# Nineteen taps of a depthwise convolution moved from VectorE to ScalarE products and accumulating transfers, in a two-layer encoder on one core

## The chip, the cores and the metric

The kernel runs on 1 core of one Trainium2 chip. The metric is device microseconds (us) of one execution, less is better. The kernel before takes 1756.23 us, the median of 3 runs (1755.57 to 1756.38).

## The reference, cut to what matters

Two layers of an encoder over 512 tokens of 1024 channels, in float32. Each layer projects the normalized tokens, runs three token mixers side by side (a: differential attention with 4 heads, b: a Conformer convolution module, c: neighbourhood attention with 8 heads), weighs each mixer's output by a sigmoid gate, adds the three, and goes on with an output projection, a SwiGLU feed-forward block and a gated embedding. The two places that the change touches are the convolution and the sum of the branches:

```python
def conformer_conv(u, conv_w, conv_b, cln_g, cln_b):
    a, g = jnp.split(u, 2, axis=-1)
    z = a * jax.nn.sigmoid(g)
    z = lax.conv_general_dilated(
        z, conv_w.astype(z.dtype), window_strides=(1,),
        padding=[(CONV_W // 2, CONV_W // 2)],
        dimension_numbers=('NWC', 'WIO', 'NWC'),
        feature_group_count=CB)
    z = z + conv_b
    z = layernorm(z, cln_g, cln_b)
    return jax.nn.silu(z)
...
        merged = (ga * (ya @ w_br_a[i]) + gb * (yb @ w_br_b[i])
                  + gc * (yc @ w_br_c[i]))
```

The convolution has 31 taps (`CONV_W`) and one weight for each tap and channel, over 512 channels (`CB`). The channels lie on the partitions in 4 blocks of 128, so one tap of one block is one pass over a 128x512 tile: multiply a shifted view of the block by a column of weights and add it to the sum. A layer has 4 x 31 = 124 such passes.

## The kernel before, in words

**Products on TensorE.** Activations lie with channels on the partitions and 512 tokens along the free side. A float32 product is made of three matmuls of halves: each weight tile `wr` is loaded by SyncE, ScalarE copies its high part to `wh` (helper `act`, L143), VectorE subtracts to get the low part `wl` (helper `tt`, L157), and `mm3` (L179, L180, L181) issues high x high, high x low, low x high. `weights` does the loading and splitting with raised priority, up to 400 steps ahead of its use; `wr`, `wh` and `wl` have three buffers each.

**Order.** TensorE's order is the program's order, written out by hand (`manual_schedule`). The streams of the other engines are put in order when the kernel is built, by priority and an estimate of when each instruction's inputs are there; a link that is only an order (`NoSync`) holds an instruction behind another one. Within an engine instructions run in that fixed order, and an instruction that waits holds all that are behind it. Attention units (`natten_unit`, `diff_unit`) are put between the projections by counting matmul chunks (`tick`, `later`): a unit's scores (L800) go to two PSUM buffers `sc`; VectorE takes the maximum (L893), ScalarE the exponential of both tiles (`diff_a`, `diff_e`, L143), VectorE mixes them (L898 and L160), and three ticks later TensorE transposes the result.

**The taps.** `taps` is a generator over the 124 passes; each `yield` is one VectorE `scalar_tensor_tensor` (helper `stt`, L160) or, for a block's first tap, one `tensor_scalar` (L551). `background(after, n)` takes the next `n` of them and puts them behind the instruction `after`. `BG` tells how many go where: 4 in the stage `glu`, 8 in `natten`, 12 in the neighbourhood values, 8 in `diff`, 16 in `gatec`, 16 in `branchc`, 16 behind the four first gates of b, and 48 in `mergea` (6 for each of 8 blocks), which is 80 places before `mergea` and 128 in all. What is left is done at the start of `conv`, which adds the four sums, and normalizes them over the channels.

**Stages of a layer around the change.** `diff_in` for heads 0 to 3 projects q and k of one head each: ScalarE copies the PSUM result to `raw` (tile `diff_rp`), four SyncE transfers rotate it, VectorE applies the rotary tables, ScalarE and VectorE split it, SyncE transfers stack it. `gate_c` projects one of 8 gate blocks and copies it (tile `gatec_x`); block 0 stands between heads 1 and 2, blocks 1 to 7 behind head 3. Then `branch_c` (gate times product of branch c, in place in `acc`), `merge_a` (gate of a times product of branch a into `g`, then `acc += g`, two VectorE instructions per block), `conv` with the rest of the gates of b, and `merge_b`, which is the next to read `acc`.

**Transfers that add.** The feed-forward block has them already: two for each of its 44 weight blocks, issued from GpSimd (`accum_op=ALU.add`, L979), which add 128x512 weights from HBM to a tile in SBUF. GpSimd has little else to do: the power -0.5 of the norms (L225, L1334).

**The buffers that the change uses.** Tiles of tag `z` are as large as 128x1024, so a 128x512 sum fills half of one. The tag `rb` has one buffer, which holds a norm's factor for all tokens; between the start of the layer and the convolution's norm it is free.

Of the kernel before, what the change touches and what calls it, by code (L numbers as in the profile page):

```python
# [14 lines left out]
AF = mybir.ActivationFunctionType  # L15
ALU = mybir.AluOpType
# [4 lines left out]
P = 128  # L21
# [3 lines left out]
GR = 8  # L25
# [4 lines left out]
CB = 512  # L30
CON3W = 31
HALO = CON3W // 2
NA_KR = 8
NA_KC = 16
NW = 256
# [10 lines left out]
PAR_L = 8 + 8 + 8 + 1 + 4 + 4 + 4 + 4 * CON3W  # L46
PAR = L * PAR_L + 8
WARM = 8
BG = dict(glu=2, natten=1, values=3, diff=1, gatec=2, branchc=2, gateb=4, mergea=4, mergea2=2)
FIRST = (["v"] * 4 + ["pt"] * 2 + ["y", "b"], ["y"] * 5 + ["pt"] * 2 + ["b"])  # L50
EARLY = 6
QUARTERS = (2, 4, 6)
# [9 lines left out]
class Net:  # L62
# [371 lines left out]
    def layer(self, i, h, xsrc, xs):  # L434
        self.i, self.h = i, h
        zs, cs = [], []
        self.todo = self.taps(zs, cs)
        self.glu(zs)
        if i == 0:
            self.lambdas()  # L440
        yc, ya, yb = [], [], []
        sn, sd = {}, {}
        self.natten_in(0, sn, yc)
        self.drain(self.renorm)
        self.h = self.hs
        self.natten_v(sn)
        last = self.glu_last(zs)
        self.natten_in(1, sn, yc)
        next(last)
        self.natten_in(2, sn, yc)  # L450
        next(last)
        self.natten_in(3, sn, yc)
        acc, gb = [], []
        self.diff_in(0, sd, ya)
        self.diff_v(0, sd)
        self.diff_in(1, sd, ya)
        self.gate_c(acc, 0)
        self.diff_in(2, sd, ya)
        self.diff_v(1, sd)
        self.diff_in(3, sd, ya)  # L460
        for m in range(1, KD):
            self.gate_c(acc, m)
        for m in range(2):
            self.gate_b(gb, m, AF.Copy, None)
        for g in acc + gb:
            self.act(g, g, AF.Sigmoid, table="sigmoid")
        self.branch_c(acc, yc)
        for m in range(2, 4):
            self.gate_b(gb, m, AF.Sigmoid, "sigmoid")
        self.merge_a(ya, acc)  # L470
        conv = self.run(self.conv(cs, yb))
        pairs = self.inputs()
        for m in range(4, KD):
            self.gate_b(gb, m, AF.Sigmoid, "sigmoid")
            for n in ((0, 1), (2,), (3,), ())[m - 4]:
                self.input_block(pairs, n)
        self.drain(conv)
        mg = self.merge_b(yb, acc, gb)
        ws = self.pair_weights(4)
        x, h = self.w_o(mg, xsrc)  # L480
        self.input_pair(ws, pairs, 4)
        h = self.ffn(h, x)
        return self.ple(h, x, xs, self.inputs())
# [8 lines left out]
    def glu(self, zs):  # L492
# [5 lines left out]
        for j in range(3):  # L498
            sg, ta = self.sb("t", [P, 512]), self.sb("t", [P, 512])
            z = self.sb("z", [P, GW + 2 * HALO, GR])  # L500
            zs.append(z)
# [17 lines left out]
    def gated(self, z, a, g):  # L519

        nc = self.nc
        zc = self.tt(z[:, HALO:HALO + GW, :].rearrange("p a b -> p (a b)"), a, g, ALU.mult)
        nc.vector.memset(z[:, 0:HALO, 0:1], 0.0)
        nc.vector.memset(z[:, HALO + GW:, GR - 1:GR], 0.0)
        nc.vector.tensor_copy(z[:, 0:HALO, 1:GR], z[:, GW:GW + HALO, 0:GR - 1])
        nc.vector.tensor_copy(z[:, HALO + GW:, 0:GR - 1], z[:, HALO:2 * HALO, 1:GR])
        return zc
# [13 lines left out]
    def taps(self, zs, cs):  # L541

        for j, z in enumerate(zs):
            zf = z.rearrange("p a b -> p (a b)")
            c = self.sb("z", [P, 512])
            cs.append(c)
            for d in range(CON3W):
                w = self.par(self.i, "cw", j * CON3W + d)
                src = zf[:, d * GR:d * GR + 512]
                if d == 0:  # L550
                    yield self.nc.vector.tensor_scalar(c, src, w, self.par(self.i, "cb", j),  # L551
                                                       ALU.mult, ALU.add)
                else:
                    yield self.stt(c, src, w, c, ALU.mult, ALU.add)

    def background(self, after, n):

# [193 lines left out]
    def gate_c(self, acc, m):  # L751
        self.phase = "gatec"
        ps = self.proj(OFF_G + 2 * D + m * P)
        if m % 2 == 0:
            acc += self.parts_of("x", [512], 2)
        self.background(self.act(acc[m], ps, AF.Copy), self.bg["gatec"])

    def branch_c(self, acc, ys):
        self.phase = "branchc"
        for m in range(KD):  # L760
            ps = self.ps("mm")
            self.gemm(ps, self.a["w_br_c"][self.i, m], ys)
            self.background(self.tt(acc[m], acc[m], ps, ALU.mult), self.bg["branchc"])

    def merge_a(self, ys, acc):
        self.phase = "mergea"
        for m in range(KD):
            ps = self.proj(OFF_G + m * P)
            g = self.sb("t", [P, 512])
            self.background(self.act(g, ps, AF.Sigmoid, table="sigmoid"), self.bg["mergea"])  # L770
            pb = self.ps("mm")
            self.gemm(pb, self.a["w_br_a"][self.i, m], ys)
            self.tt(g, g, pb, ALU.mult)
            self.background(self.tt(acc[m], acc[m], g, ALU.add), self.bg["mergea2"])

    def gate_b(self, gs, m, func, table):
        self.phase = "gateb"
# [24 lines left out]
    def diff_in(self, head, st, ys):  # L802
        self.phase = "diff"
        if head == 0:
            st["tabs"] = []
            for t in range(2):
                c = self.sb("r", [P, 512])
                self.nc.sync.dma_start(c, self.a["rope"][t])
                st["tabs"].append(c)
        st4 = self.sb("qk", [P, 4, 512], F32R)  # L810
        k2 = self.sb("x", [P, 2, 512], F32R)
        for s, off in enumerate((OFF_QA, OFF_KA)):
            ps = self.proj(off + head * P)
            raw, rot = self.sb("rp", [P, 512]), self.sb("rp", [P, 512])
            self.act(raw, ps, AF.Copy, scale=1.0 if s else 0.125)
            for b in range(4):
                o = b ^ 1
                self.nc.sync.dma_start(rot[32 * b:32 * b + 32], raw[32 * o:32 * o + 32])
            t = self.sb("t", [P, 512])
            self.background(self.tt(t, raw, st["tabs"][0], ALU.mult), self.bg["diff"])  # L820
            self.tt(rot, rot, st["tabs"][1], ALU.mult)
            self.tt(t, t, rot, ALU.add)
            nat, low = self.sb("kh", [P, 512], F32R), raw.bitcast(F32R)
            self.split(nat, low, t)
            self.stack(nat, low, st4[:, 2 * s:2 * s + 2], k2 if s else None)
        box = dict(s0=self.sb("sm", [P, 4]))
        for qt in range(4):
            self.later(self.diff_unit(head, qt, st4, k2, st, box, ys), 6 if head else 7, 2)
# [693 lines left out]
```

## Time and profile before

| | before |
|---|---|
| median of 3 runs | 1756.23 us |
| the profiled execution's own time | 1756.09 us |
| its span, from the first to the last instruction | 1754.3 us |
| PE, matmuls | 1747.3 us busy, 8970 instructions |
| PEld, weight loads | 1490.2 us busy |
| DVE (VectorE) | 1421.7 us busy, 81% |
| ACT (ScalarE) | 964.4 us busy, 55% |
| POOL (GpSimd) | 104.0 us busy, 6% |
| mean granted clock of TensorE | 0.999 |

The profiled execution lies 0.14 us under the median, and its span leaves 1.8 us of its time uncovered. A row of a timeline reads: start in us from the span's start, duration in us, engine, line, operation, output tile and inputs, shape, count; in square brackets, the idle time of the engine just before and who ended it. In a view by tile the three durations are minimum, median and maximum in ns. Matmul rows are modelled at their ends and overlap: the distance from one start to the next tells TensorE's pace, not the duration. In the rows of windows the numbers after an engine are busy us and instructions.

### The profile page before, as it was taken

Reading aid. Unit: us, or ns where it says so; the run is one execution under the profiler, and the core shown is the slowest. Engines: PE = TensorE matmul, PEld = TensorE weight load, DVE = VectorE, ACT = ScalarE, POOL = GpSimd, SP = SyncE. Lnnn points to the kernel's source line nnn. Section 1 sums busy time; section 2 is a strip of 40 time slices with the busy share of each in tenths; the row PEclk is TensorE's granted clock in tenths of the full one; section 3 lists DMA queues with packets and bytes.
Section 4 is the critical chain, followed back from the end, with each engine's and each line's share of the span. In section 5 each row is a group of like instructions: output and inputs, shape, how many; then the busy total and the mean of one; then the engine's idle time right before and its main releaser. Section 6 shows DMA issues by size and latency. Waiting matters only on the chain.

```text
span 1754.3 us, 25072 instructions
## 1 busy us (share of the span) xinstructions
PE 1747.3 (100%) x8970; PEld 1490.2 (85%) x8970; DVE 1421.7 (81%) x2346; ACT 964.4 (55%) x1729; POOL 104.0 (6%) x114
## 2 busy tenths in 40 slices
PE   9999999999999999999999999999999999999998
PEld 7888888888888888888888898888888988888887
DVE  7967987998799687797776688889887985977876
ACT  5566545226577275574545665553365763745654
POOL 0000000000121020100000000000001210101000
PEclk9999999999999999999999999999999999999999
DMA  6575641334767365543446655323256764755332
GB/s 230 159 192 158 162 126 46 112 100 140 230 162 186 118 171 155 142 119 131 156 130 164 194 150 153 111 73 96 93 176 199 183 172 121 179 143 157 96 105 97
DMA packets 114781, 253.82 MB, mean 145 GB/s; under 512 B 16864, under 2 KB 23776, under 8 KB 114656
## 3 DMA queue, kind: packets, MB, share of 16 engines
q1 hardware_dynamic: 101264, 227.83, 42.3%
q0 software_dynamic: 12672, 23.07, 8.1%
q8 instruction: 71, 1.16, 0.3%
q10 hardware_dynamic: 720, 1.31, 0.2%
q14 instruction: 54, 0.44, 0.1%
HBM read 215.46 MB, written 7.34 MB: 127 GB/s over the span
## 4 chain that ended last, share of the span: by engine, by line
PE 97%; DVE 1%; DMA 1%; ACT 1%; SPq 0%; issue 0%; POOL 0%; POOLq 0%; ACTq 0%; DVEq 0%
PE ffn_mm L1013 6%; PE ffn_sc L1013 6%; PE ffn_mm L180 4%; PE ffn_mm L179 4%; PE ffn_mm L181 4%; PE ffn_mm L1016 3%; PE ffn_sc L1016 3%; PE mergea_mm L180 2%; PE mergea_mm L181 2%; PE mergea_mm L179 2%; PE ffn_tr L1013 2%; PE natten_mm L179 2%; PE natten_mm L180 2%; PE gateb_mm L180 2%; PE gateb_mm L181 2%; PE gateb_mm L179 2%
## 5 line engine op out<-in xcount | busy, mean ns | idle before, releaser
L160 DVE SCALAR_TENSOR_TENSOR conv_z<-glu_z,pre_par,conv_z 128x512 f32<-128x512 f32 x240 | 179.6, 748 | 3.4
L143 ACT ACTIVATE ffn_wh<-ffn_wr 128x1024 fp32r<-128x1024 f32 (+1 forms) x92 | 92.7, 1021 | 99.5 <-PE ffn_mm L180 63.4
L157 DVE TENSOR_TENSOR ffn_wl<-ffn_wr,ffn_wh 128x1024 fp32r<-128x1024 f32 (+1 forms) x92 | 107.1, 1175 | 20.8 <-ACT ffn_wh L143 20.4
L979 POOL DMA_DIRECT2D ffn_qk<-w_fu x88 | 78.0, 992 | 589.3 <-DMA ffn_qk<-w_fu 323.7
L143 ACT ACTIVATE mergea_wh<-mergea_wr 128x1024 fp32r<-128x1024 f32 (+1 forms) x32 | 27.1, 846 | 96.8 <-PE mergea_mm L180 79.6
L157 DVE TENSOR_TENSOR ffn_t<-ffn_mm,wo_rb 128x512 f32<-128x512 f32 (+1 forms) x46 | 31.1, 677 | 51.6 <-PE ffn_mm L181 51.6
L157 DVE TENSOR_TENSOR ffn_wl<-ffn_qk,ffn_wh 128x1024 fp32r<-128x1024 f32 x44 | 53.7, 1220 | 11.0 <-ACT ffn_wh L143 10.9
L143 ACT ACTIVATE diff_a<-diff_sc,diff_s 128x512 f32<-128x512 f32 x32 | 22.0, 688 | 71.6 <-DVE diff_s L893 71.6
L143 ACT ACTIVATE ffn_wh<-ffn_qk 128x1024 fp32r<-128x1024 f32 x44 | 46.7, 1061 | 26.8 <-PE ffn_mm L180 16.2
L179 PE MATMUL ffn_mm<-ffn_v,ffn_wh 128*128 128x512 f32 x132 | 51.4, 389 | 0.0
L180 PE MATMUL ffn_mm<-ffn_v,ffn_wh 128*128 128x512 f32 x132 | 51.4, 389 | 0.0
L181 PE MATMUL ffn_mm<-ffn_v,ffn_wl 128*128 128x512 f32 x132 | 51.3, 389 | 0.0
L179 PE MATMUL ffn_mm<-ffn_y,ffn_wh 128*128 128x512 f32 x132 | 51.3, 389 | 0.0
L180 PE MATMUL ffn_mm<-ffn_y,ffn_wh 128*128 128x512 f32 x132 | 51.3, 389 | 0.0
L181 PE MATMUL ffn_mm<-ffn_y,ffn_wl 128*128 128x512 f32 x132 | 51.3, 389 | 0.0
L143 ACT ACTIVATE natten_wh<-natten_wr 128x1024 fp32r<-128x1024 f32 x24 | 25.4, 1058 | 42.2 <-issue 15.5
L1013 PE MATMUL ffn_sc<-wo_h,ffn_wh 128*128 128x512 f32 x176 | 48.0, 394 | 0.0
L157 DVE TENSOR_TENSOR ffn_t<-ffn_t,ffn_e 128x256 f32<-128x256 f32 x84 | 46.3, 551 | 1.0 <-ACT ffn_e L143 0.9
L893 DVE TENSOR_REDUCE diff_s<-diff_sc 128x1 f32<-128x512 f32 x64 | 42.1, 683 | 2.2 <-PE diff_sc L800 2.2
L1013 PE MATMUL ffn_mm<-wo_h,ffn_wh 128*128 128x512 f32 x160 | 43.6, 394 | 0.0
L225 POOL TENSOR_TENSOR diff_rc<-diff_sm,pre_power 128x4 f32<-128x4 f32 x8 | 8.9, 1115 | 561.8 <-DVE diff_sm L160 503.2
L143 ACT ACTIVATE natten_b<-natten_b,natten_s 128x256 f32<-128x256 f32 x64 | 30.4, 499 | 20.4 <-DVE natten_s L719 20.3
(894 smaller groups left out, 6050.1 us busy)
## 6 DMA issues: line engine op xcount, KB each, us to landing
ffn_qk<-w_fu POOLq DMA_DIRECT2D x88, 256.0 KB, 6.6
ffn_wr<-w_fg SPq DMA_DIRECT2D x44, 512.0 KB, 4.4
ffn_wr<-w_fd SPq DMA_DIRECT2D x32, 448.0 KB, 3.8
ffn_r<-w_fu SPq DMA_DIRECT2D x44, 256.0 KB, 3.1
ffn_qk<-w_fg SPq DMA_DIRECT2D x44, 256.0 KB, 3.3
ffn_qk<-w_fu SPq DMA_DIRECT2D x44, 256.0 KB, 3.4
natten_wr<-w_in SPq DMA_DIRECT2D x16, 512.0 KB, 4.2
diff_wr<-w_in SPq DMA_DIRECT2D x16, 512.0 KB, 4.3
```

Of the source, the lines that this page charges most:

```text
L143: i = self.nc.scalar.activation(out, in_, func, **kw)
L157: return self.nc.vector.tensor_tensor(out, a, b, op)
L160: return self.nc.vector.scalar_tensor_tensor(out, a, s, b, op0, op1)
L179: mm(out, wh, ah, start=first, stop=False, **kw)
L180: mm(out, wh, al, start=False, stop=False, **kw)
L181: mm(out, wl, ah, start=False, stop=last, **kw)
L225: nc.gpsimd.tensor_tensor(col, ms, self.power, ALU.pow)
L893: nc.vector.tensor_reduce(out=m[:, u:u + 1], in_=sc, op=ALU.max, axis=AX.X, negate=True)
L979: nc.gpsimd.dma_start(q, wu[:, lo], accum_op=ALU.add)
L1013: mm(out, wh[:, c], bs[k][b], start=first and k == 0, stop=False, skip_group_check=True)
L1016: mm(out[:, 0], wl[:, c], bs[k][b][:, 0], start=False, stop=k == 3, skip_group_check=True)
```

## The change

Two things are changed, in both layers. First, of the convolution's last block (j = 3) the first 19 taps (`ASIDE`) are no longer VectorE's. The new generator `aside` makes them one by one: the first is a ScalarE activation with scale and bias into a second sum `half[0]` (the second half of a `z` tile), each of the other 18 is a ScalarE product into the one tile `t` (tag `rb`) and a GpSimd transfer that adds `t` to `half[0]`. The next product writes `t` again, so it waits until that transfer has landed. `beside(after)` takes one product and puts it behind `after`: in `diff_in` twice for each head (behind the copies of q and of k), behind each of the 8 gate copies in `gate_c`, and in `branch_c` at blocks 0, 3 and 6 behind the newest weight split. That is 8 + 8 + 3 = 19 places. The remaining 12 taps stay on VectorE, and the first of them takes `half[0]` as its addend. Second, `merge_a` no longer adds on VectorE: a GpSimd transfer adds `g` to `acc[m]`. The places for taps in `mergea` go from 4 + 2 to 3 + 1 for each block, so that there are 112 places for 105 taps.

```diff
+ASIDE = 19
...
-BG = dict(glu=2, natten=1, values=3, diff=1, gatec=2, branchc=2, gateb=4, mergea=4, mergea2=2)
+BG = dict(glu=2, natten=1, values=3, diff=1, gatec=2, branchc=2, gateb=4, mergea=3, mergea2=1)
...
-        self.todo = self.taps(zs, cs)
+        self.half = {}
+        self.todo, self.other = self.taps(zs, cs), self.aside(zs)
...
-            c = self.sb("z", [P, 512])
+            c, self.half[j] = self.parts_of("z", [512], 2)
             cs.append(c)
-            for d in range(CON3W):
+            for d in range(ASIDE if j == 3 else 0, CON3W):
                 w = self.par(self.i, "cw", j * CON3W + d)
                 src = zf[:, d * GR:d * GR + 512]
-                if d == 0:
+                if j == 3 and d == ASIDE:
+                    for _ in self.other:
+                        pass
+                    yield self.stt(c, src, w, self.half[0], ALU.mult, ALU.add)
+                elif d == 0:
                     yield self.nc.vector.tensor_scalar(c, src, w, self.par(self.i, "cb", j),
                                                        ALU.mult, ALU.add)
                 else:
                     yield self.stt(c, src, w, c, ALU.mult, ALU.add)
+
+    def aside(self, zs):
+
+        zf = zs[3].rearrange("p a b -> p (a b)")
+        c, t = self.half[0], self.sb("rb", [P, 512])
+        for d in range(ASIDE):
+            w = self.par(self.i, "cw", 3 * CON3W + d)
+            src = zf[:, d * GR:d * GR + 512]
+            if d == 0:
+                yield self.act(c, src, AF.Identity, scale=w, bias=self.par(self.i, "cb", 3))
+            else:
+                i = self.act(t, src, AF.Copy, scale=w)
+                self.nc.gpsimd.dma_start(c, t, accum_op=ALU.add)
+                yield i
+
+    def beside(self, after):
+
+        ph, self.phase = self.phase, "conv"
+        i = next(self.other, None) if 0 in self.half else None
+        if i is not None:
+            self.behind(i, after)
+        self.phase = ph
...
-        self.background(self.act(acc[m], ps, AF.Copy), self.bg["gatec"])
+        last = self.act(acc[m], ps, AF.Copy)
+        self.background(last, self.bg["gatec"])
+        self.beside(last)
...
-            self.background(self.tt(acc[m], acc[m], ps, ALU.mult), self.bg["branchc"])
+            last = self.tt(acc[m], acc[m], ps, ALU.mult)
+            self.background(last, self.bg["branchc"])
+            if m % 3 == 0:
+                self.beside(self.low)
...
-            self.tt(g, g, pb, ALU.mult)
-            self.background(self.tt(acc[m], acc[m], g, ALU.add), self.bg["mergea2"])
+            self.background(self.tt(g, g, pb, ALU.mult), self.bg["mergea2"])
+            self.nc.gpsimd.dma_start(acc[m], g, accum_op=ALU.add)
...
-            self.act(raw, ps, AF.Copy, scale=1.0 if s else 0.125)
+            last = self.act(raw, ps, AF.Copy, scale=1.0 if s else 0.125)
...
             self.stack(nat, low, st4[:, 2 * s:2 * s + 2], k2 if s else None)
+            self.beside(last)
```

## The prediction, made before the changed kernel ran

> **What bounds the kernel now.** I read the page's first part, then TensorE's waits, then four windows, two for each layer: from the first copy of `diff_in` to the end of `branch_c`, and from there to the end of `merge_a`. The columns of a window are us, then busy us and instructions of PE, PEld, DVE, ACT, POOL, then granted clock, DMA share, GB/s.
>
> ```profile
> span 1754.3 us, 25072 instructions
> PE 1747.3 (100%) x8970; PEld 1490.2 (85%) x8970; DVE 1421.7 (81%) x2346; ACT 964.4 (55%) x1729; POOL 104.0 (6%) x114
> ```
> ```profile
> PE pre_av L331 <- DVE pre_zeror L404: 1.1, 1, 1.1
> PE diff_sc L800 <- ACT diff_e L143: 0.2, 1, 0.2
> ```
> ```profile
> 134.00:312.00 178.00, 177.77 (x1005) 154.40 (x1004) 147.51 (x266) 99.50 (x207) 4.47 (x4) 1.00 0.44 122
> 312.00:394.00 82.00, 82.00 (x363) 67.93 (x362) 75.58 (x103) 23.68 (x33) 0.00 (x0) 1.00 0.32 101
> ...
> 1003.00:1180.00 177.00, 177.00 (x1003) 154.31 (x1002) 147.34 (x267) 100.04 (x209) 4.46 (x4) 1.00 0.44 124
> 1180.00:1263.00 83.00, 83.00 (x367) 68.74 (x367) 76.16 (x104) 23.68 (x33) 0.00 (x0) 1.00 0.32 100
> ```
>
> TensorE is the bound, and the view of waits says more than the share of busy time, which is modelled. Over the whole span it names two waits, 1.1 us at the very start and 0.2 us in the first layer's attention: 1.3 us in all. In the window of `merge_a` 363 matmuls fill 82.00 us, 0.226 us each, and 367 fill 83.00 us in the second layer, 0.226 again, at a granted clock of 1.00. So TensorE does not wait for VectorE even where VectorE is busiest (75.58 of 82 us, 92%). The change touches no matmul. What it takes from VectorE can shorten the time by what TensorE waits for, of which only the 0.2 us lie in the stages touched. The question is whether it adds a wait.
>
> **What is removed.** The tap, in its group on the page; the addition of `merge_a` and a block's first tap, in the views of their tiles:
>
> ```profile
> L160 DVE SCALAR_TENSOR_TENSOR conv_z<-glu_z,pre_par,conv_z 128x512 f32<-128x512 f32 x240 | 179.6, 748 | 3.4
> ```
> ```profile
> L157 DVE TENSOR_TENSOR gatec_x<-gatec_x,mergea_t x16: 684/687/689, 340.0 to 1264.2; 128x512 f32<-128x512 f32 x16
> ```
> ```profile
> L551 DVE TENSOR_SCALAR conv_z<-glu_z,pre_par x8: 532/543/548, 36.5 to 1220.8; 128x512 f32<-128x512 f32 x8
> ```
>
> VectorE loses 18 x 0.748 and the block's first tap (L551, 0.543), 14.0 us, and 8 x 0.687 = 5.5 us: 19.5 us in a layer, 39.0 us in all. In the window of `merge_a` it loses 16 places for taps and 8 additions, 12.0 + 5.5 = 17.5 of its 75.58 us. On TensorE's path all this is worth nothing, because no wait for VectorE ends there: 0, at most the 0.2 us.
>
> **What ScalarE gets.** The nearest rows: a copy of the same shape with a column as its scale, and an activation with columns as scale and bias, both from SBUF.
>
> ```profile
> L143 ACT ACTIVATE wo_t<-wo_x,pre_par x16: 706/708/713, 462.9 to 1361.0; 128x512 f32<-128x512 f32 x16
> ...
> L143 ACT ACTIVATE conv_t<-conv_z,pre_par x8: 797/809/818, 413.5 to 1289.7; 128x512 f32<-128x512 f32 x8
> ```
>
> 18 x 0.708 + 0.809 = 13.6 us in a layer. They fall in the window in which ScalarE is busy 99.50 of 178 us, so it goes to 113.1, 64%. The cover of one product is ScalarE's idle time before the next exponential, where it waits for VectorE's maximum. In the stretch where the scores have least to spare, head 1 of layer 0:
>
> ```profile
> 165.38 0.59 ACT L143 ACTIVATE diff_rp<-diff_mm 128x512 f32<-128x512 f32 x1
> ...
> 171.28 0.69 ACT L143 ACTIVATE diff_a<-diff_sc,diff_s 128x512 f32<-128x512 f32 x1 [3.38 <-DVE diff_s L893]
> ...
> 175.56 0.58 ACT L143 ACTIVATE diff_rp<-diff_mm 128x512 f32<-128x512 f32 x1
> ...
> 179.42 0.69 ACT L143 ACTIVATE diff_a<-diff_sc,diff_s 128x512 f32<-128x512 f32 x1 [2.66 <-DVE diff_s L893]
> ...
> 189.01 0.60 ACT L143 ACTIVATE gatec_x<-gatec_mm 128x512 f32<-128x512 f32 x1
> 189.49 0.61 ACT L143 ACTIVATE diff_rp<-diff_mm 128x512 f32<-128x512 f32 x1
> 193.84 0.69 ACT L143 ACTIVATE diff_a<-diff_sc,diff_s 128x512 f32<-128x512 f32 x1 [3.74 <-DVE diff_s L893]
> ...
> 195.46 0.67 ACT L143 ACTIVATE diff_e<-diff_sc,diff_s 128x512 f32<-128x512 f32 x1
> ```
>
> The products of head 1 go behind the copies at 165.38 and 175.56; 0.71 us disappears in idle times of 3.38 and 2.66 us. A product by itself costs 0; without that cover it would cost up to its 0.708 us in each of the few places where the scores come close behind.
>
> **What the transfers cost.** The feed-forward block's transfers that add are of the same 128x512 shape, with the source in HBM; their issue on GpSimd and the time from issue to landing:
>
> ```profile
> L979 POOL DMA_DIRECT2D ffn_qk<-w_fu x88: 862/886/1248, 448.0 to 1621.0; - x88
> ...
> DMA to landing us min/median/max: 4.0/6.6/9.8
> ```
> ```profile
> q1 hardware_dynamic: 101264, 227.83, 42.3%
> q0 software_dynamic: 12672, 23.07, 8.1%
> ```
>
> No transfer that adds from SBUF is in the trace; 4.0 and 9.8 us are the ends, and I take 5.0, nearer to the least, since these go out singly and their windows have a DMA share of 0.44 and 0.32. GpSimd gets 18 + 8 = 26 issues of 0.886 us in a layer, 23 us. Queue q0 took 8.1% of 1754.3 us for 23.07 MB, so 6.2 us of all 16 DMA engines for 1 MB, 1.6 us for each 0.262 MB: 18 of them raise the share of the first window from 0.44 to 0.60 (29 of 178 us), 8 raise that of `merge_a` from 0.32 to 0.48. The queues do not fill.
>
> GpSimd's queue also holds the powers of the norms, which now may stand behind an issue:
>
> ```profile
> 276.48 1.01 POOL L225 TENSOR_TENSOR diff_rc<-diff_sm,pre_power 128x4 f32<-128x4 f32 x1 [30.14 <-DVE diff_sm L160]
> ```
> ```profile
> 282.02 0.60 PE L229 MATMUL diff_tr<-pre_ident,diff_rc 128*128 128x128 f32 x4
> ```
>
> The power ends at 277.49 and TensorE reads it at 282.02: 4.5 us cover an issue of 0.9. ```profile
> L143 ACT ACTIVATE mergeb_y<-gatec_x x10: 616/619/636, 427.7 to 1309.0; 128x512 fp32r<-128x512 f32 x10
> ```
> ```profile
> 307.39 0.69 DVE L157 TENSOR_TENSOR branchc_wl<-branchc_wr,branchc_wh 128x512 fp32r<-128x512 f32 x1
> ...
> 351.99 0.54 DVE L551 TENSOR_SCALAR conv_z<-glu_z,pre_par 128x512 f32<-128x512 f32 x1
> ...
> 395.47 0.69 DVE L157 TENSOR_TENSOR gatec_x<-gatec_x,mergea_t 128x512 f32<-128x512 f32 x1
> ```
>
> Nobody waits for the sums soon. `merge_b` reads `acc` from 427.7 on; the last addition of `merge_a` begins at 395.47, and a landing 9.8 us later is 405. The partial sum `half[0]` has as much room: its last product goes behind the split at 307.39, and the last block's taps begin at 351.99 now, and later than that with fewer places, so 44 us.
>
> **The wait that is added.** A product overwrites `t`, so it waits for the landing before it, on ScalarE, and holds ScalarE's stream. The first three places quoted lie 10 and 13 us apart. The next pair does not: at 189 the copies of gate block 0 and of head 2 follow each other within 0.48 us, and each brings a product. Where the second one stands in the stream is not told by the trace. If it stands right behind the copy at 189.49, it goes thus: first product to 189.61 + 0.71 = 190.32, landing at 195.32 with 5.0 us, second product to 196.03, and then the exponentials, which began at 193.84; the second one, which ended at 196.13, ends 2.19 later, at 198.32. TensorE wants the two buffers again here:
>
> ```profile
> 196.56 0.40 PE L800 MATMUL diff_sc<-diff_qk 128*128 128x512 f32 x1
> ...
> 197.03 0.39 PE L800 MATMUL diff_sc<-diff_qk 128*128 128x512 f32 x1
> ```
>
> That is 1.3 us late. In layer 1 the same place:
>
> ```profile
> 1057.12 0.61 ACT L143 ACTIVATE diff_rp<-diff_mm 128x512 f32<-128x512 f32 x1
> 1061.47 0.69 ACT L143 ACTIVATE diff_a<-diff_sc,diff_s 128x512 f32<-128x512 f32 x1 [3.74 <-DVE diff_s L893]
> ...
> 1063.09 0.68 ACT L143 ACTIVATE diff_e<-diff_sc,diff_s 128x512 f32<-128x512 f32 x1
> ```
> ```profile
> 1065.79 0.39 PE L800 MATMUL diff_sc<-diff_qk 128*128 128x512 f32 x1
> ```
>
> The copy of the gate lies as far ahead of this one as in layer 0, so the first product ends about 1057.95, lands at 1062.95, the second ends at 1063.66, and the second exponential moves by 2.19 from 1063.77 to 1065.96: 0.2 us late. Together 1.5 us with 5.0; with 6.6 it is 2.9 + 1.8 = 4.7 us, with 4.0 it is 0.3 us, with 9.8 it is 11.1 us. It is 0 if the stream has other work ahead of the second product. Gate blocks 6 and 7 are a second such pair, but the exponentials stand within 1 us of it, sooner than any landing, so a product that waits there is likely behind them and costs nothing:
>
> ```profile
> 283.58 1.09 ACT L143 ACTIVATE gatec_x<-gatec_mm 128x512 f32<-128x512 f32 x2 [3.41 <-PE diff_sc L800]
> 284.55 0.69 ACT L143 ACTIVATE diff_a<-diff_sc,diff_s 128x512 f32<-128x512 f32 x1
> ```
>
> By the Trainium skill, page "DMA: Bandwidth & Descriptors", section "Anatomy of one DMA — SWDGE (gpsimd) path", such a transfer takes 2.0 us and its bytes at 436 GB/s; my estimate from it is 2.6 us for 0.262 MB. By that the second product would be done at 193.6, ahead of the exponential, and the wait would cost nothing. The least landing in the trace is 4.0 us, so the trace does not agree for a transfer that adds, and the sum goes by the trace.
>
> **The sum.** Removed 0; products 0; transfers 0; the wait 0 to 1.5, of which I take the half, 0.8 us. The profiled execution of 1756.09 goes to 1756.9, and at the median, 0.14 higher, to 1757.0. Each layer has this once; there is nothing else on the path.
>
> **Rivals.** *ScalarE's stream stands at the second product with long landings.* One mechanism, the place above, and it decides when that product is queued ahead of the exponentials and the landing takes 6.6 us, as the median does, or more. For it: the median row, and that the stream is ordered by an estimate made at the build, while the landing is whatever it is on the chip. Against it: other transfers run in the feed-forward block by twos behind each other, here one by one. 4.7 us, so 1760.9; with 9.8 us 1767.3. Chance 0.30.
>
> *The new transfers push the others.* Head 1's rotations and stackings run while its products' transfers do, and the only wait in these stages, 0.2 us for `diff_e`, shows that layer 0 has no slack there. One transfer's 1.6 us of all engines in each layer is 3.2 us: 1759.4. Against it: a share of 0.60 leaves gaps. Chance 0.08. The Trainium skill says in the same page, section "Issuing engines are not separate DMA queues", that transfers issued from GpSimd run on the same 16 engines as SyncE's and interleave with them; that is the rule against this change, and the two shares are what the trace has on it.
>
> *The relief shows.* VectorE's 19.5 us per layer would have to end a wait, and 0.2 us is all there is: 1756.0. Chance 0.02 for more than I can see, faster.
>
> **How the numbers follow.** The forecast, no change that shows, has 0.60. A measurement of this kernel can tell about 0.2%, 3.5 us. Same: 0.60, with 0.08 of the pushed transfers and 0.05 of the first rival, where the landing lies below 6 us: 0.73. Slower: the rest of the first rival, 0.25. Faster: 0.02. The range reaches from 1755.5, half a us under the gain's end, to 1765.0, which takes in the first rival up to landings of about 8.5 us; beyond lie about 0.08.
>
> **What would show it.** Right: TensorE's waits stay under 3 us in all, `merge_a` still runs at 0.226 us per matmul with VectorE near 58 of 82 us, ScalarE's products take 0.71 us, and the windows of `diff_in` to `branch_c` keep 178 and 177 us within 2. The first rival shows as a wait of TensorE's L800 for `diff_e` of some us near 196 and 1065, and ScalarE idle before a product until a transfer. The second shows as waits for `diff_rp` or `diff_x` transfers. I am wrong if TensorE waits in `merge_a` or the convolution, or if the span shortens by more than 2 us.

## The result, and the profile after

The changed kernel takes 1770.49 us (median of 4 runs, 1768.53 to 1772.3), the kernel before 1755.9 (median of 4, 1755.54 to 1756.38): 14.6 us more, a ratio of 1.0083 [1.0065, 1.01]. The runs of after lie 3.8 us apart, those of before 0.8. The profiled execution of after is the shortest of its four, 1768.53 us with a span of 1766.8; its span is 12.5 us longer than that of before, and it is these 12.5 us that the trace can show.

The page of after, its first part, the queue of GpSimd's transfers, the group of the new transfers, and their issues with the median us to landing:

```profile
span 1766.8 us, 25198 instructions
...
PE 1751.1 (99%) x8970; PEld 1490.8 (84%) x8970; DVE 1385.5 (78%) x2292; ACT 987.9 (56%) x1767; POOL 150.0 (8%) x166
...
q0 software_dynamic: 20160, 36.71, 12.8%
...
L573 POOL DMA_DIRECT2D conv_z<-conv_rb x36 | 32.0, 888 | 489.4 <-ACT conv_rb L144 489.1
...
conv_z<-conv_rb POOLq DMA_DIRECT2D x36, 256.0 KB, 4.0
```

TensorE still has its 8970 matmuls, in the same order, and is busy for 3.8 us more than before; the rest of the 12.5 us is idle time. VectorE is relieved as the change says, from 1421.7 to 1385.5 us. The 36 transfers of the taps land after 4.0 us in the median, below the 5.0 that the prediction took. TensorE's waits (us in total, times, longest):

```profile
PE diff_tr L216 <- ACT diff_ss L144: 4.1, 2, 2.9
PE diff_sc L833 <- ACT diff_e L144: 2.1, 2, 1.2
PE diff_sc L833 <- DMA diff_rp<-diff_rp: 1.8, 2, 0.9
PE pre_av L332 <- DVE pre_zeror L405: 1.1, 1, 1.1
PE diff_sc L833 <- ACT diff_a L144: 0.6, 2, 0.4
PE natten_sc L833 <- PE diff_mm L653: 0.3, 1, 0.3
PE diff_av L181 <- DVE diff_pt L158: 0.2, 1, 0.2
```

Before there were two rows, `pre_av` and 0.2 us for `diff_e`. The four large ones beside `pre_av` lie in the attention of branch a. Three of them name ScalarE; the fourth names a transfer, and the rows below show that it is ScalarE as well. The four windows, cut at the same work as before (us, then busy us and instructions of PE, PEld, DVE, ACT, POOL, clock, DMA share, GB/s):

```profile
134.00:316.00 182.00, 176.62 (x992) 152.43 (x991) 145.12 (x262) 110.51 (x225) 20.51 (x22) 1.00 0.57 142
316.00:398.00 82.00, 82.00 (x365) 67.89 (x364) 60.84 (x82) 24.06 (x33) 6.20 (x8) 1.00 0.48 122
1011.00:1189.00 178.00, 174.31 (x977) 150.22 (x976) 143.23 (x256) 109.23 (x221) 19.00 (x21) 1.00 0.57 143
1189.00:1272.00 83.00, 83.00 (x370) 68.75 (x369) 62.36 (x84) 24.34 (x34) 7.58 (x9) 1.00 0.46 119
```

In `merge_a` nothing has changed for TensorE: 365 matmuls in 82.00 us, 0.225 us each, with VectorE down from 75.58 to 60.84. In the stages from `diff_in` to `branch_c` it is idle for 5.4 us in the first layer and 3.7 in the second. The shares of the DMA engines are 0.57, where 0.60 was predicted, and 0.48, as predicted.

Where the idle time comes in shows best when the start of the same matmul is read in both traces (us from the span's start):

| matmul | before | after | later by | since the row above |
|---|---|---|---|---|
| `natten_av`, layer 0 | 165.81 | 166.53 | 0.72 | 0.72 |
| `diff_sc` of head 1, layer 0 | 175.19 | 176.97 | 1.78 | 1.06 |
| `diff_sc` behind the pair, layer 0 | 197.03 | 200.56 | 3.53 | 1.75 |
| `diff_tr` of `diff_ss`, layer 0 | 303.54 | 310.28 | 6.74 | 3.21 |
| `natten_sc`, layer 1 | 1024.59 | 1031.86 | 7.27 | 0.53 |
| `diff_sc` of head 1, layer 1 | 1044.21 | 1053.03 | 8.82 | 1.55 |
| `diff_av`, layer 1 | 1061.84 | 1071.33 | 9.49 | 0.67 |
| `diff_sc` behind the pair, layer 1 | 1065.79 | 1076.85 | 11.06 | 1.57 |
| `diff_tr` of `diff_ss`, layer 1 | 1172.31 | 1184.83 | 12.52 | 1.46 |

Three kinds of place hold it all: the pair of gate block 0 and head 2 (1.75 + 1.57 = 3.3 us), the sum `diff_ss` of the last attention unit in `branch_c` (3.21 + 1.46 = 4.7 us), and the stretch of heads 0 and 1 (the other five rows, 4.5 us, of which 0.3 us are there already at 5.16 us, long before the stages that the change touches; so 4.2 us).

**The pair.** ScalarE's timeline of after, layer 0:

```profile
191.14 0.60 ACT L144 ACTIVATE gatec_x<-gatec_mm 128x512 f32<-128x512 f32 x1
191.62 0.73 ACT L144 ACTIVATE conv_rb<-glu_z,pre_par 128x512 f32<-128x512 f32 x1
192.24 0.60 ACT L144 ACTIVATE diff_rp<-diff_mm 128x512 f32<-128x512 f32 x1
197.50 0.72 ACT L144 ACTIVATE conv_rb<-glu_z,pre_par 128x512 f32<-128x512 f32 x1 [4.66 <-DMA conv_z<-conv_rb]
198.13 0.67 ACT L144 ACTIVATE diff_a<-diff_sc,diff_s 128x512 f32<-128x512 f32 x1
...
199.74 0.68 ACT L144 ACTIVATE diff_e<-diff_sc,diff_s 128x512 f32<-128x512 f32 x1
```

The second product waits for the first one's landing, 5.15 us from the end of the first (192.35) to its start, and the exponential `diff_a`, whose maximum VectorE had ended at 196.53, begins only behind it. TensorE's rows there:

```profile
198.94 0.50 PE L833 MATMUL diff_sc<-diff_qk 128*128 128x512 f32 x1 [0.39 <-ACT diff_a L144]
...
200.56 0.50 PE L833 MATMUL diff_sc<-diff_qk 128*128 128x512 f32 x1 [0.88 <-DMA diff_rp<-diff_rp]
```

The first waits for `diff_a`. The second is put down to a transfer of `diff_rp`, but `diff_e` ended at 199.74 + 0.68 = 200.42 and this row begins 0.14 later, as the row at 198.94 begins 0.14 after the end of `diff_a` (198.13 + 0.67). So the 1.8 us of the third row of the waits belong to the pair as well; the releaser in the brackets is only the event that came last by the records.

**The product ahead of `diff_ss`.** ScalarE in `branch_c`, after, and TensorE's row behind it:

```profile
301.91 0.72 ACT L144 ACTIVATE conv_rb<-glu_z,pre_par 128x512 f32<-128x512 f32 x1
...
309.02 0.72 ACT L144 ACTIVATE conv_rb<-glu_z,pre_par 128x512 f32<-128x512 f32 x1 [5.40 <-DMA conv_z<-conv_rb]
309.65 0.58 ACT L144 ACTIVATE diff_ss<-diff_av 128x512 f32<-128x512 f32 x1
```
```profile
310.28 0.66 PE L216 MATMUL diff_tr<-pre_ident,diff_ss 128*128 128x128 f32 x4 [2.93 <-ACT diff_ss L144]
```

The product at 309.02, the second of the three in `branch_c`, waits 5.40 us for the landing before it. (The layer's last product, at 314.05, holds up nothing that TensorE waits for.) Behind it in ScalarE's stream is `diff_ss` of the last attention unit, and TensorE's transposes wait for that. Before, it was issued as soon as its input was there:

```profile
300.99 0.60 ACT L143 ACTIVATE diff_ss<-diff_av 128x512 f32<-128x512 f32 x1 [1.03 <-PE diff_av L181]
```

**Heads 0 and 1.** VectorE multiplies the rotated tile as soon as SyncE's four transfers are there. The rows of head 0's k and of head 1's q in layer 0, before:

```profile
148.71 0.69 DVE L157 TENSOR_TENSOR diff_rp<-diff_rp,diff_r 128x512 f32<-128x512 f32 x1 [0.73 <-DMA diff_rp<-diff_rp]
...
173.03 0.69 DVE L157 TENSOR_TENSOR diff_rp<-diff_rp,diff_r 128x512 f32<-128x512 f32 x1 [1.79 <-DMA diff_rp<-diff_rp]
```

The same two after, and the maximum that stands behind the second:

```profile
149.92 0.69 DVE L158 TENSOR_TENSOR diff_rp<-diff_rp,diff_r 128x512 f32<-128x512 f32 x1 [1.71 <-DMA diff_rp<-diff_rp]
...
174.81 0.69 DVE L158 TENSOR_TENSOR diff_rp<-diff_rp,diff_r 128x512 f32<-128x512 f32 x1 [2.36 <-DMA diff_rp<-diff_rp]
175.42 0.69 DVE L927 TENSOR_REDUCE diff_s<-diff_sc 128x1 f32<-128x512 f32 x1
```

No product waits here; ScalarE's wait for `diff_s` is the wait for this maximum. What is late is the rotation: VectorE waits 1.0 and 0.6 us longer than before. The second row is 1.78 us late, and most of that, 1.21 us, is there at the first row already.

### The profile page after: what moved, and what is told of

It reads as the page before. It is cut to its first block, busy times and chain, and to the rows that moved or that the text cites. A ratio compares the mean times of both kernels' runs of the same rounds, so it can differ in the third digit from the quotient of the medians.

```text
span 1766.8 us, 25198 instructions
## 1 busy us (share of the span) xinstructions
PE 1751.1 (99%) x8970; PEld 1490.8 (84%) x8970; DVE 1385.5 (78%) x2292; ACT 987.9 (56%) x1767; POOL 150.0 (8%) x166
## 4 chain that ended last, share of the span: by engine, by line
PE 91%; DMA 3%; ACT 3%; DVE 2%; issue 1%; SPq 1%; POOL 0%; ACTq 0%; DVEq 0%; POOLq 0%
PE ffn_mm L1047 6%; PE ffn_sc L1047 6%; PE ffn_mm L180 4%; PE ffn_mm L182 4%; PE ffn_mm L181 4%; PE ffn_mm L1050 3%; PE ffn_sc L1050 3%; PE mergea_mm L180 2%; PE mergea_mm L182 2%; PE mergea_mm L181 2%; PE ffn_tr L1047 2%; PE natten_mm L181 2%; PE natten_mm L180 2%; PE natten_mm L182 2%; PE wo_mm L181 2%; PE wo_mm L182 2%
## 5 line engine op out<-in xcount | busy, mean ns | idle before, releaser
L161 DVE SCALAR_TENSOR_TENSOR conv_z<-glu_z,pre_par,conv_z 128x512 f32<-128x512 f32 x204 | 152.5, 747 | 2.9
L573 POOL DMA_DIRECT2D conv_z<-conv_rb x36 | 32.0, 888 | 489.4 <-ACT conv_rb L144 489.1
L158 DVE TENSOR_TENSOR ffn_wl<-ffn_qk,ffn_wh 128x1024 fp32r<-128x1024 f32 x44 | 53.8, 1222 | 11.0 <-ACT ffn_wh L144 10.9
L158 DVE TENSOR_TENSOR mergea_wl<-mergea_wr,mergea_wh 128x1024 fp32r<-128x1024 f32 (+1 forms) x32 | 30.7, 959 | 31.8 <-ACT mergea_wh L144 30.7
```

What stands on the lines that cost most here:

```text
L158: return self.nc.vector.tensor_tensor(out, a, b, op)
L161: return self.nc.vector.scalar_tensor_tensor(out, a, s, b, op0, op1)
L573: self.nc.gpsimd.dma_start(c, t, accum_op=ALU.add)
```

## The experiments

*Theory 1*: the loss is made at those places. At two of them a product that waits for a landing holds ScalarE's stream, and with it what TensorE wants; at heads 0 and 1 the new transfers make the rotations land later. *Theory 2*: it is the load, that is, the products on ScalarE, or the transfers as such, each of which costs about the same wherever it stands. The first four kernels were measured beside 30 runs of before (median 1756.17 us), the next four beside 13 (1755.7), the last four beside 31 (1756.08).

**Half of the change at a time.** The relief alone: before, with the 19 taps gone and nothing in their place.

```diff
-BG = dict(glu=2, natten=1, values=3, diff=1, gatec=2, branchc=2, gateb=4, mergea=4, mergea2=2)
+BG = dict(glu=2, natten=1, values=3, diff=1, gatec=2, branchc=2, gateb=4, mergea=3, mergea2=1)
...
-            for d in range(CON3W):
+            for d in range(19 if j == 3 else 0, CON3W):
...
-                if d == 0:
+                if d == (19 if j == 3 else 0):
```

> The kernel before with the first 19 taps of the convolution's last block left out and nothing in their place (the block's sum starts at tap 19), and 4 places for taps in each block of merge_a instead of 6. It is the relief of VectorE without any of its price. If TensorE never waits for VectorE in these stages, the time stays where it was, 1755.9 us within 0.5. If the relief itself is worth something, it is faster by more than 1 us, and the change has lost that much more than it shows.

1755.78 us (1755.39 to 1756.36), 0.9999 [0.9989, 1.0008]. Fourteen us less of VectorE in each layer buy nothing.

`merge_a`'s additions by transfers alone:

```diff
-            self.tt(g, g, pb, ALU.mult)
-            self.background(self.tt(acc[m], acc[m], g, ALU.add), self.bg["mergea2"])
+            self.background(self.tt(g, g, pb, ALU.mult), self.bg["mergea2"])
+            self.nc.gpsimd.dma_start(acc[m], g, accum_op=ALU.add)
```

> Only the second half of the change: merge_a's additions by transfers, all 124 taps on VectorE in the places of before. My theory, that the loss comes from ScalarE's stream and from the rotations in the attention stages, has nothing here: 1755.9 us within 0.5, TensorE's pace in merge_a 0.226 us per matmul. The rival, that transfers which add disturb TensorE or the weights' loads by themselves, has 16 of the 52 new transfers here and would give a third of the 14.6 us, about 1760.

1756.63 us (1755.98 to 1757.37), 1.0002 [0.9992, 1.0011]: these 16 transfers cost nothing. All of the loss is made by the taps.

After with the products, but without the taps' transfers:

```diff
                 i = self.act(t, src, AF.Copy, scale=w)
-                self.nc.gpsimd.dma_start(c, t, accum_op=ALU.add)
                 yield i
```

> The changed kernel with all 19 products on ScalarE and the 18 transfers of the taps left out (the sum half[0] holds the first product alone); merge_a's transfers stay. A product waits for nothing but its place. Theory 1: the products' 13.6 us per layer disappear in ScalarE's idle time, 1756 to 1757. Theory 2, ScalarE's load: it stays above 1762.

1756.36 us (1755.73 to 1757.08), 1.0001 [0.9991, 1.001]. ScalarE carries all 38 products, and nothing is lost: theory 2 falls for ScalarE's load. It takes the transfers.

After with a new tile for each product, so that no product waits for the landing before it:

```diff
-        c, t = self.half[0], self.sb("rb", [P, 512])
+        c = self.half[0]
...
             else:
+                t = self.sb("t", [P, 512])
                 i = self.act(t, src, AF.Copy, scale=w)
```

> The changed kernel with a tile of its own for each product (from the ring t of seven) in place of the one tile, so that a product need not wait for the landing of the transfer before it; the transfers still follow each other. Theory 1, ScalarE's stream held by that wait at the pair near 192 us and at the last product in branch_c: those losses go (1.8 + 3.1 us in layer 0, 1.6 + 1.4 in layer 1, 7.8 of 12.5 in the profiled spans), and what is left is the rotations pushed by the transfers and small change, 1760 to 1763. Theory 2, the load of products and transfers itself: it stays at 1768 to 1772.

1760.99 us (1759.52 to 1762.88), 1.0028 [1.0017, 1.0038]. TensorE's waits:

```profile
PE pre_av L332 <- DVE pre_zeror L405: 1.1, 1, 1.1
PE diff_sc L834 <- ACT diff_e L144: 1.0, 2, 0.8
PE diff_av L181 <- DVE diff_pt L158: 0.3, 1, 0.3
PE diff_tr L216 <- ACT diff_ss L144: 0.2, 1, 0.2
PE diff_tr L230 <- DVE diff_pt L158: 0.2, 1, 0.2
```

The wait for `diff_ss` is down from 4.1 to 0.2 us. Of the 14.6 us about 9.8 are gone (14.6 less 4.8), with all 36 transfers still there: up to two thirds are the wait for the tile. It may be less, because ScalarE's order changed as well: the product at head 0's k in layer 0 now stands further back, its transfer starts 2.1 us after that rotation's first issue instead of 0.7, and the rotation's last transfer lands 6.2 us after that issue instead of 7.7. The 4.8 us that stay are not the wait for the tile.

**Places taken out one after the other.** After without products in `branch_c`:

```diff
-ASIDE = 19
+ASIDE = 16
...
-            if m % 3 == 0:
-                self.beside(self.low)
```

> After with 16 taps aside instead of 19, none of them in branch_c; the three taps go back to VectorE; the products at the heads and at the gates stay as they are. Theory 1 (a product that waits for a landing holds what is queued behind it on ScalarE; the last product holds diff_ss and so the transposes near 303 and 1172): only that place goes, 3.1 + 1.4 = 4.4 us, so 1766.0 us; TensorE's wait for diff_ss is gone, those for diff_e near 197 and 1065 stay at 1 to 2 us. Theory 2 (each transfer costs about the same, wherever it stands): 15 of 18 transfers are left, 14.6 x 15/18 = 12.2 us over before, 1768.1 us.

1765.81 us (1765.22 to 1769.21), 1.0062 [1.0047, 1.0077]: by the medians 4.7 us less than after; theory 1 had 1766.0. That the table has 4.7 us at `diff_ss` too is in part luck, since the four runs of either kernel lie 4 us apart, and against theory 2's 1768.1 the time alone does not decide. The trace does for the mechanism: TensorE has no wait for `diff_ss` left in it.

Without gate block 0 as well, so that there is no pair:

```diff
-ASIDE = 19
+ASIDE = 15
...
-        self.beside(last)
+        if m:
+            self.beside(last)
...
-            if m % 3 == 0:
-                self.beside(self.low)
```

> After with 15 taps aside: none in branch_c and none at gate block 0, so that no product stands within 9 us of the one before it among the heads. Theory 1: the places at diff_ss (4.4 us) and at the pair (1.8 + 1.6 us) go; what is left are the rotations pushed by transfers, as with a tile for each product, 4.8 to 6.8 us over before: 1761 to 1763 us. Theory 2: 14 of 18 transfers are left, 14.6 x 14/18 = 11.4 us over before, 1767.3 us.

1764.23 us (1763.84 to 1765.15), 1.005 [1.0033, 1.0067]: 1.2 us above theory 1's upper end and 3 below theory 2. ScalarE waits for landings 2.2 us in all, none of them longer than 0.9 us, where after has 21.1 us, and this kernel still loses 8.5 us, so the rotations cost more than I took from the table. The places are not additive: taking the pair away gave 1.6 us where the table has 3.3. Lateness at one place that covers lateness at the next would explain it; no run shows that.

Only heads 0 and 1 (4 taps), with `merge_a`'s transfers and with as many places for taps as before:

```diff
-ASIDE = 19
+ASIDE = 4
...
-BG = dict(glu=2, natten=1, values=3, diff=1, gatec=2, branchc=2, gateb=4, mergea=3, mergea2=1)
+BG = dict(glu=2, natten=1, values=3, diff=1, gatec=2, branchc=2, gateb=4, mergea=4, mergea2=2)
...
-        self.beside(last)
...
-            if m % 3 == 0:
-                self.beside(self.low)
...
-            self.beside(last)
+            if head < 2:
+                self.beside(last)
```

> After with 4 taps aside, at the copies of q and k of heads 0 and 1 alone; merge_a's additions by transfer stay. Theory 1: what is left is the late rotations of head 1, 1.0 us in layer 0 and 0.5 to 1.2 us in layer 1, so 1757.5 to 1758.5 us. Theory 2: 3 of 18 transfers, 2.4 us over before, 1758.6 us. If it is the same as before, the late rotations are not made by the transfer just ahead of them but by several transfers together or by the products.

1762.88 us (1762.28 to 1764.64), 1.0043 [1.0028, 1.0057]. Both theories were far off: three transfers in each layer lose 7.2 us, half of the whole loss.

Only gate blocks 1 to 7 (7 taps), the rest likewise:

```diff
-ASIDE = 19
+ASIDE = 7
...
-        self.beside(last)
+        if m:
+            self.beside(last)
...
-            if m % 3 == 0:
-                self.beside(self.low)
...
-            self.beside(last)
```

> After with 7 taps aside, at gate blocks 1 to 7 alone; merge_a's additions by transfer stay. Theory 1: there the exponentials are ahead of each product that waits and no rotation is under way, so no loss: 1756.2 us within 0.7, and no gain either. Theory 2: 6 of 18 transfers, 4.9 us over before, 1761.1 us.

1755.88 us (1755.36 to 1756.43), 1.0 [0.999, 1.0009]: six transfers in each layer lose nothing. With this pair theory 2 is gone: three transfers in one place cost 7.2 us and six in another none.

**Why heads 0 and 1.** If it is the rotation, the same four taps must be free where rotations have slack.

```diff
-            if head < 2:
+            if head >= 2:
                 self.beside(last)
```

> The same 4 taps aside as with heads 0 and 1 alone (1762.9 us), but at the copies of q and k of heads 2 and 3; merge_a's additions by transfer stay. Theory 1a (a transfer beside a rotation makes the rotation land 2 to 3 us later, and only the rotations of heads 0 and 1 have no slack): the rotations of heads 2 and 3 land later as well, and nothing waits: 1756.2 us within 1. Theory 1b (every transfer beside a rotation costs TensorE about 1 us): 3 transfers in each layer as before, 1762 us.

1755.53 us (1755.32 to 1757.53), 1.0 [0.999, 1.0009]. The rotations of heads 2 and 3 did become later. The four transfers of head 2's k in layer 0, us from issue to landing, before and in this kernel:

```profile
DMA to landing us min/median/max: 2.4/3.1/3.7
```
```profile
DMA to landing us min/median/max: 3.4/3.8/3.9
```

The least, the median and the largest are 1.0, 0.7 and 0.2 us more, and from the first issue to the last landing it is 5.7 us instead of 4.3. VectorE, which reads them at 203.82, 1.7 us after the last landing, does not wait (no brackets):

```profile
203.82 0.68 DVE L158 TENSOR_TENSOR diff_rp<-diff_rp,diff_r 128x512 f32<-128x512 f32 x1
```

So theory 1a: what counts is the slack of the rotation beside the transfer. Before, this rotation landed 3.1 us ahead of its reader, while VectorE's only three waits for rotations are at head 0's k and head 1's q in layer 0 and at head 1's q in layer 1. But the push is also smaller here, 1.5 us where head 0's k with its transfer has 2.4 (9.2 instead of 6.7 us in the run with heads 0 and 1), so slack need not be the whole difference. What of the transfer pushes it was asked with two kernels that have the same order on every engine as the one with heads 0 and 1 alone. Copies instead of additions:

```diff
-                self.nc.gpsimd.dma_start(c, t, accum_op=ALU.add)
+                self.nc.gpsimd.dma_start(c, t)
```

> 4 taps aside at heads 0 and 1, as in the run of 1762.9 us and in the same order on every engine, but the transfers copy the product over the sum instead of adding it: the sum of these taps is left out. Theory 1c (adding is what makes the transfer push the rotations): 1756 to 1758 us. Theory 1d (any transfer of 256 KB from GpSimd does it): 1762.9 us within 1.

1759.23 us (1757.39 to 1763.12), 1.002 [1.001, 1.0029]: 3.1 us over before, between the two. Adding makes it worse, but copying does it too.

Additions of few bytes:

```diff
-                self.nc.gpsimd.dma_start(c, t, accum_op=ALU.add)
+                self.nc.gpsimd.dma_start(c[:, :32], t[:, :32], accum_op=ALU.add)
```

> 4 taps aside at heads 0 and 1, as in the run of 1762.9 us and in the same order on every engine, but each transfer adds only 32 of the 512 columns (16 KB instead of 256 KB): 480 columns of three taps are left out of the sum. Theory 1e (the bytes of the transfer push the rotations): 1756 to 1757 us. Theory 1f (its issue on GpSimd or its number of packets, which stay, do): 1762 to 1763 us.

1756.08 us (1755.36 to 1756.82), 0.9999 [0.999, 1.0008]: nothing is lost. The issues on GpSimd are the same, and so are the packets of queue q0; the bytes are not. The rows of q0 for additions, copies and few bytes (packets, MB, share of 16 engines):

```profile
q0 software_dynamic: 15840, 28.84, 10.2%
```
```profile
q0 software_dynamic: 15456, 28.84, 9.9%
```
```profile
q0 software_dynamic: 15840, 27.37, 9.8%
```

The rotation that is hit first is that of head 0's k in layer 0, four transfers of 64 KB from SyncE: duration of the issues (ns, minimum, median, maximum), then us to landing. Before, with additions, with few bytes:

```profile
L818 SPq DMA_DIRECT2D diff_rp<-diff_rp x4: 507/558/594, 141.8 to 144.2; - x4
...
DMA to landing us min/median/max: 1.9/4.3/4.8
```
```profile
L848 SPq DMA_DIRECT2D diff_rp<-diff_rp x4: 507/558/1803, 143.0 to 145.4; - x4
...
DMA to landing us min/median/max: 1.9/6.2/7.1
```
```profile
L848 SPq DMA_DIRECT2D diff_rp<-diff_rp x4: 507/558/592, 142.4 to 144.8; - x4
...
DMA to landing us min/median/max: 1.9/3.9/4.4
```

With additions the slowest of them lands after 7.1 us instead of 4.8, 2.3 more, and one issue of SyncE takes 1.8 us instead of 0.6; with few bytes neither happens. Of the 64 such issues in a whole trace 2 are longer than 1 us before, 8 with additions, 2 with copies and 2 with few bytes. VectorE's wait for the rotations over the whole span (us, times, longest), before, with additions, copies and few bytes:

```profile
DVE diff_rp L157 <- DMA diff_rp<-diff_rp: 3.2, 3, 1.8
```
```profile
DVE diff_rp L158 <- DMA diff_rp<-diff_rp: 11.1, 6, 3.2
```
```profile
DVE diff_rp L158 <- DMA diff_rp<-diff_rp: 7.3, 4, 2.5
```
```profile
DVE diff_rp L158 <- DMA diff_rp<-diff_rp: 2.6, 3, 1.3
```

11.1, 7.3 and 2.6 us go with a loss of 7.2, 3.1 and 0 us. Before has 3.2 us of this wait, and TensorE waits 0.2: in these four some 3 to 4 us are covered, and what is beyond shows on TensorE. It is no rule for other orders: the same row has 13.8 us in the kernel without `branch_c` and without the pair (8.5 us lost) and 10.9 us in the one with a tile for each product (4.8 us lost).

**All three places left out.** Heads 2 and 3 and gate blocks 1 to 7, one tile for all products, places for taps as with heads 0 and 1 alone:

```diff
-ASIDE = 19
+ASIDE = 11
...
-        self.beside(last)
+        if m:
+            self.beside(last)
...
-            if m % 3 == 0:
-                self.beside(self.low)
...
-            self.beside(last)
+            if head >= 2:
+                self.beside(last)
```

> 11 taps aside with the one tile: at heads 2 and 3 and at gate blocks 1 to 7; none at heads 0 and 1, at gate block 0 and in branch_c; merge_a's additions by transfer stay. Theory 1 (the loss is made at three places: late rotations of heads 0 and 1, the pair of gate block 0 and head 2, diff_ss behind the last product): all three are gone, 1756.2 us within 1, with 10 of 18 transfers left. Theory 2 (each transfer costs): 14.6 x 10/18 = 8.1 us over before, 1764 us. No theory expects it below before.

1756.55 us (1755.33 to 1758.35), 1.0002 [0.9992, 1.0011]: ten transfers in each layer and no loss that can be told, and no gain. The profiled execution, at 1758.35 the longest, has one late rotation left, that of head 3's k in layer 1, and TensorE waits 1.1 us for `diff_ss` and 0.4 us for `diff_pt` behind it, so the later heads have slack, but not always enough. No version that was run beats the kernel before, and none can be expected to by this way: what it frees is VectorE, and before, TensorE waits for VectorE only once, at the very start.

## Why the prediction was wrong

**The bound: right.** TensorE bounds the kernel before and after. What was taken from VectorE is worth 0, as predicted: 0.9999 [0.9989, 1.0008] with the taps left out.

**The products: right.** The rows of the timeline have them at 0.72 to 0.73 us, and without their transfers they cost nothing (1.0001 [0.9991, 1.001]). The transfers of `merge_a` cost nothing either (1.0002 [0.9992, 1.0011]). The pair of gate blocks 6 and 7 is free, as predicted: with products at gate blocks 1 to 7 alone the time is that of before.

**The pair: the right place and mechanism, mis-sized.** The prediction had 1.3 us for layer 0 and 0.2 for layer 1, and took half. The second product does stand ahead of the exponentials, and TensorE lost 1.75 and 1.57 us there. In layer 0 the landing was as taken (5.15 us from product to product) and the size nearly right. In layer 1 the step that failed is "so the first product ends about 1057.95". The two copies stayed as close as in layer 0, but they lost their lead over the attention: the copy of the gate began at 1068.35 instead of 1056.64, 11.7 us later, while the matmul that opens the stretch, `diff_av` at 1061.84, was 9.5 us later. It had been held by a late `diff_kh`, whose rotation came late, and so the pair stood 2.2 us closer to the exponentials than worked out; the landing was shorter there (4.24 us from product to product), which took back a part.

**The products in `branch_c`: the step that failed with no rival beside it.** "Its last product goes behind the split at 307.39 ... so 44 us" asks who reads the sum, and answers rightly. It does not ask who stands behind a product on ScalarE. The prediction had asked that question for the pair and not for the other products that share the tile. Three of them stand in `branch_c`, and behind the second, which waits for the first one's landing, is `diff_ss`, with TensorE waiting for it: 4.7 us by the table, which no rival named. Leaving these products out gave 4.7 us back by the medians.

**The pushed rotations: named as a rival, with a chance of 0.08 and one transfer's 1.6 us a layer.** In the sum the transfers stand at 0, and that term failed; it is the largest when the places are left out one after the other. "A share of 0.60 leaves gaps" was the reason for it. The share came out at 0.57 and says nothing on it: three rotations had no slack before, and one addition of 256 KB beside head 0's k makes the slowest of its transfers land after 7.1 us instead of 4.8. More than one place in a layer pays: 7.2 us with three transfers a layer. The rule that stood beside this rival, of the Trainium skill, page "DMA: Bandwidth & Descriptors", section "Issuing engines are not separate DMA queues", agrees with the runs: a transfer issued from GpSimd delays SyncE's, and with a sixteenth of the bytes it does not. The 2.6 us that the prediction estimated from the section "Anatomy of one DMA — SWDGE (gpsimd) path" of the same page do not agree for transfers that add: the least of the 36 landings is 3.2 us, the median 4.0 and the largest 6.7.

**The sum.** "Each layer has this once; there is nothing else on the path" was wrong twice over. By leaving out one after the other, the 14.6 us are 4.7 in `branch_c`, 1.6 at the pair and 7.7 at heads 0 and 1 (1764.23 less 1756.55, where the runs of before beside them differ by 0.4), with 0.5 left. What stays open is how these split when all are there: the table of starts gives 4.7, 3.3 and 4.2, a tile for each product gave back 9.8 us where the two places that wait for the tile have 6.3 by leaving out, and no run separates how lateness at one place covers the next. Why an addition pushes more than a copy of the same bytes is not settled either; q0 has 15840 packets and a share of 10.2% against 15456 and 9.9%, which fits engines that are held longer, and only additions stretch SyncE's issues (8 of 64 over 1 us against 2); no run shows more.

## What to carry to other kernels

When an instruction gets a wait for a transfer, look down its engine's stream from that instruction to the first one that somebody waits for, at every place where it is put, and not only at the reader of its result. A mean share of the DMA engines does not tell whether a transfer may be put beside another: find the small transfers that somebody waits for, read their slack, and keep large ones away from them. And when the engine that bounds the kernel never waits for another one in the stages touched, taking work from that other engine is worth nothing there (14 us of VectorE's in each layer changed nothing here), so that any price on the way is the whole effect.

## What the runs showed of the hardware

Transfers of 256 KB that add from SBUF to SBUF land after 3.2, 4.0 and 6.7 us (least, median, largest of 36), sooner than those that add from HBM in the feed-forward block of before (median 6.6). The six at heads 0 and 1 took 3.9 to 6.6 us, five of them more than 5.8; the eight at heads 2 and 3 took 3.2 to 5.1. With additions at heads 0 and 1, 8 of SyncE's 64 issues for rotations took more than 1 us, against 2 of 64 before, so a part of the delay begins ahead of the landing. A long issue alone is no sign of it: before has one of 1.8 us too, without any such transfer. An addition is 144 packets of queue q0 and a copy of the same tile 80 (worked out from the packets of the page: 2304 more for `merge_a`'s 16 alone, and 384 fewer with 6 copies in place of 6 additions), and its issue on GpSimd takes 0.87 us against 0.57. The time of after scatters over 3.8 us where before scatters over 0.8, which would fit a time that hangs on when transfers land; no run tests that.
